# Four of the mixer's norms: squares added by block transposes on DVE and one 33-column matmul, 1 / rms on 32 partitions, spread by way of DRAM

## The chip, the cores and the metric

The kernel runs on one core of a Trainium2 chip. Its time is the device time of one execution in microseconds; the median of three runs was 1979.41 us. The engines are TensorE (PE; its weight loads are shown apart as PEld), VectorE (DVE), ScalarE (ACT), GpSimd (POOL) and SyncE (SP). In this kernel SP issues nearly all DMAs, from one queue in order.

## What is computed

One step of a decoder layer over 16 meta tokens, 1024 prompt tokens and 8 sample tokens, 1048 in all: a SwiGLU half step, a mixer of two head groups, an output projection, a second SwiGLU half step, a final norm. The change is in the mixer, in the norm of each HGRN2 head (four heads of 128 channels) and of each Mamba-2 group (two groups of 256 channels), cut from the reference:

```python
    o_hg = o_hg * lax.rsqrt(jnp.mean(o_hg * o_hg, axis=-1, keepdims=True) + EPS)
    o_hg = o_hg.reshape(bsz, seqlen, HG_WIDTH) * hg_norm.astype(f32) * jax.nn.silu(g.astype(f32))
    ...
    yz = (y.reshape(bsz, seqlen, SSM_WIDTH) * jax.nn.silu(z.astype(f32))).reshape(bsz, seqlen, SSM_GROUPS, -1)
    yz = yz * lax.rsqrt(jnp.mean(yz * yz, axis=-1, keepdims=True) + EPS)
    yz = yz.reshape(bsz, seqlen, SSM_WIDTH) * ssm_norm.astype(f32)
    ...
    mix = jnp.concatenate([o_hg, yz], axis=-1).astype(h.dtype) @ w_out
```

## The kernel before

**Layout.** Channels lie on the 128 partitions and tokens along the free dimension, so each norm is a sum over partitions, wanted on every partition for 1032 tokens (the meta tokens are dropped; `TO` = 1032).

**A norm.** `hgrn_out` (L1816) gets one head's output in three pieces of PSUM (496, 512 and 24 tokens). ACT squares each into `v`, DVE multiplies each by the weight `hg_norm` and the gate `g` (L1823), then TensorE multiplies a matrix of ones with the squares, in f32 (L1828): that adds over the partitions and puts the sum on all 128. ACT scales the sum and adds eps (L1829). `rstd_wide` (L190) follows: ACT loads the table with Ln and Exp (L194), takes Ln and Exp in two halves (L199, L201), DVE makes one Newton step of three passes over 128 x 1032 (L202, L203, L204), and the result `r` multiplies the gated output (L1831). `ssm_norm` (L1571) does the same for a group of two 128-channel tiles: squares (L1576, L1577), their sum (L1578), three matmuls with ones of 344 columns (L1583), `rstd_wide`, two products (L1587).

**What runs beside it.** In the mixer TensorE's order is written by hand; that of the other engines is not, and is made when the program is built. Between the steps of a scan `fill(n)` puts n steps of the input projections on TensorE: a step is one block k of 128 rows, three f32r matmuls of 344 to 350 columns (L163, L164, L165). The projections come as units in the order "q0 f0 v0 g0 q1 f1 v1 g1 z0 q2 f2 v2 g2 q3 f3 v3 z1 g3" of 24 steps each (48 for z0 and z1), 480 in all; `until(name)` runs steps until a unit is done, one step more than its last. When a unit begins, the weights of the one behind it are loaded by SP (L145, 256 KB each) and split by ACT and DVE.

**The order.** After the Mamba-2 scan, for each head hd: `fill.until("v{hd}")`, `fill(4)`, `hgrn_scan`, then for heads 0 to 2 `hgrn_out`. After head 0's come `until("z0")`, `fill(10)` and `ssm_norm` of group 0, then head 1's scan; so group 0's norm is followed by four steps of filler and a scan, and so is head 1's norm. After head 2's norm come the steps up to the end of v3 and four more. The norms of group 1 and of head 3 come at the end of the mixer. Normed outputs of heads 0 and 1 and of group 0 are written to DRAM (L2071) and read back late (L2075).

**The scan's beginning.** `hgrn_scan` transposes v on TensorE (L1650), ACT copies it (L1651), its last 8 tokens go to DRAM (`vd`, L1658) and come back spread over all partitions (L1670), for the samples' states (L1673, L1674). DVE makes q times f (L1686); TensorE makes the diagonal blocks (L1696), DVE copies them through a mask (L1700). Then come seven levels: small matmuls (L1725, from the sixth level up L1716), five filler steps, and DVE passes over q and k (L1747, L1748, L1750) on which the next level's matmuls wait. The transposes of k (L1768) follow.

Of the kernel before, what the change touches and what calls it, by code (L numbers as in the profile page):

```python
# [17 lines left out]
P = 128  # L18
D = 1024
KT = D // P  # L20
NM = 16
SEQ = 1024
TP = NM + SEQ
NS = 8
# [7 lines left out]
TO = T - NM  # L32
CHUNKS_O = [(NM, 344), (NM + 344, 344), (NM + 688, 344)]
CW = 350
SW = 1056
# [154 lines left out]
def rstd_wide(K, v, r, after):  # L190

    nc = K.nc
    with K.tc.issue_after(after.ins):
        ld = nc.scalar.preload_act_table_set("natural_log_exp_and_others")  # L194
    with K.tc.issue_after(ld.ins):
        n = v.shape[1] // 2
        parts = [(v[:, s : s + n], r[:, s : s + n]) for s in (0, n)]
        for vp, rp in parts:
            nc.scalar.activation(rp, vp, AF.Ln)  # L199
        for vp, rp in parts:  # L200
            nc.scalar.activation(rp, rp, AF.Exp, scale=-0.5, bias=K.lna)  # L201
        nc.vector.tensor_mul(v, v, r)  # L202
        nc.vector.scalar_tensor_tensor(v, v, -1.0, r, ALU.mult, ALU.mult)  # L203
        nc.vector.scalar_tensor_tensor(r, v, 3.0 * 2.0 ** (-2.0 / 3.0), r, ALU.add, ALU.mult)  # L204
# [325 lines left out]
class Inner:  # L530
# [10 lines left out]
    def next(self):  # L541
        return Inner(self.K, self.ops, self.op)
# [515 lines left out]
def constants_mix(K, a):  # L1058
    nc = K.nc
    cst = K.const  # L1060

    K.st, K.st0 = K.pack(), K.pack("u")

    K.tri = cst.tile([P, P], F32, name="tri")
    nc.gpsimd.affine_select(K.tri, K.ones[1], pattern=[[1, P]], compare_op=ALU.is_ge, fill=0.0, base=0, channel_multiplier=-1)

    K.mid = cst.tile([P, 32], U8, name="mid")
    for r in range(0, P, 32):
        nc.gpsimd.tensor_copy(K.mid[r : r + 32], K.ident[r : r + 32, r : r + 32])
    K.mask = {}  # L1070
    for m in LEVELS[:5]:
        nb = 64 // m
        f = K.sml.tile([P, 64], F32, tag="mf", name=K.uid("mf"))
        fv = f.rearrange("p (b i) -> p b i", i=m)
        on = K.ones[1][:, :64].rearrange("p (b i) -> p b i", i=m)

        nc.gpsimd.affine_select(fv, on, pattern=[[-2 * m, nb], [0, m]], compare_op=ALU.is_ge, fill=0.0, base=0, channel_multiplier=1)
        nc.gpsimd.affine_select(fv, fv, pattern=[[2 * m, nb], [0, m]], compare_op=ALU.is_ge, fill=0.0, base=m - 1, channel_multiplier=-1)
        u = cst.tile([P, 16], U8, name=f"mask{m}")
        for r in range(0, P, 32):  # L1080
            nc.gpsimd.tensor_copy(u[r : r + 32], f[r : r + 32, r // 2 : r // 2 + 16])
        K.mask[m] = u


    l0, l1 = K.pc["lb_logits"][:, 0:4], K.pc["lb_logits"][:, 4:8]
    e = K.st0.tile([P, 12])
    nc.vector.tensor_max(e[:, 8:12], l0, l1)
    nc.vector.tensor_sub(e[:, 0:4], l0, e[:, 8:12])
    nc.vector.tensor_sub(e[:, 4:8], l1, e[:, 8:12])
    nc.scalar.activation(e[:, 0:8], e[:, 0:8], AF.Exp)  # L1090
    nc.vector.tensor_add(e[:, 8:12], e[:, 0:4], e[:, 4:8])
    nc.vector.reciprocal(e[:, 8:12], e[:, 8:12])
    K.lb = cst.tile([P, 4], F32, name="lb")
    K.oml = cst.tile([P, 4], F32, name="oml")
    nc.vector.tensor_mul(K.lb, e[:, 0:4], e[:, 8:12])
    nc.vector.tensor_scalar(K.oml, K.lb, -1.0, 1.0, ALU.mult, ALU.add)

    K.dtb = K.st.tile([P, 8])
    nc.sync.dma_start(K.dtb, a["dt_bias"].to_broadcast([P, 8]))
    K.an = K.st.tile([P, 8])  # L1100
    nc.sync.dma_start(K.an, a["a_log"].to_broadcast([P, 8]))
    nc.scalar.activation(K.an, K.an, AF.Exp)
    nc.vector.tensor_scalar_mul(K.an, K.an, -1.0)
    K.dcol = K.st.tile([P, 4])
    for hf in range(2):
        nc.sync.dma_start(K.dcol[64 * hf : 64 * hf + 64, :], a["d_skip"].rearrange("l (j f) -> f l j", f=2)[hf].to_broadcast([64, 4]))

    K.sel16 = cst.tile([16, 8], F32, name="sel16")
    s2 = K.sml.tile([16, 8], F32, tag="s2", name="s2", bufs=1)
    nc.gpsimd.affine_select(K.sel16, K.ones[1][:16, :8], pattern=[[-1, 8]], compare_op=ALU.is_equal, fill=0.0, base=0, channel_multiplier=1)  # L1110
    nc.gpsimd.affine_select(s2, K.ones[1][:16, :8], pattern=[[-1, 8]], compare_op=ALU.is_equal, fill=0.0, base=-8, channel_multiplier=1)
    nc.gpsimd.tensor_add(K.sel16, K.sel16, s2)
# [455 lines left out]
    return f"z{g}", [wv[:, :, C_Z + i * P : C_Z + (i + 1) * P] for i in (2 * g, 2 * g + 1)], begin, [(i, c) for c in CHUNKS_O for i in range(2)]  # L1568


def ssm_norm(K, g, tag, fill):  # L1571

    nc = K.nc
    ya, yb = (K.y[2 * g + i][:, NM:] for i in range(2))
    v, r = K.slot(tag, w=TO), K.slot(tag, w=TO)
    nc.scalar.activation(v, ya, AF.Square)  # L1576
    nc.scalar.activation(r, yb, AF.Square)  # L1577
    nc.vector.tensor_add(v, v, r)  # L1578
    fill(10)
    for c0, w in CHUNKS_O:  # L1580
        cs = slice(c0 - NM, c0 - NM + w)
        ps = K.psm()[:, :w]
        nc.tensor.matmul(ps, K.ones[1], v[:, cs], start=True, stop=True)  # L1583
        an = nc.scalar.activation(v[:, cs], ps, AF.Identity, scale=1.0 / 256, bias=K.eps)
    rstd_wide(K, v, r, an)
    for i, y in enumerate((ya, yb)):
        nc.vector.scalar_tensor_tensor(y, y, K.pc["ssm_norm"][:, 2 * g + i : 2 * g + i + 1], r, ALU.mult, ALU.mult)  # L1587

# [227 lines left out]
def hgrn_out(K, hd, pieces, g, tag, fill):  # L1816

    nc = K.nc
    v, r = K.slot(tag, w=TO), K.slot(tag, w=TO)
    for ps, c0, w in pieces:  # L1820
        cs = slice(c0, c0 + w)
        nc.scalar.activation(v[:, cs], ps[:, :w], AF.Square)
        nc.vector.scalar_tensor_tensor(g[:, cs], ps[:, :w], K.pc["hg_norm"][:, hd : hd + 1], g[:, cs], ALU.mult, ALU.mult)  # L1823
    fill(5)
    for ps, c0, w in pieces:
        cs = slice(c0, c0 + w)
        pr = K.psm()
        nc.tensor.matmul(pr[:, :w], K.ones[1], v[:, cs], start=True, stop=True)  # L1828
        an = nc.scalar.activation(v[:, cs], pr[:, :w], AF.Identity, scale=1.0 / P, bias=K.eps)  # L1829
    rstd_wide(K, v, r, an)  # L1830
    nc.vector.tensor_mul(g, g, r)  # L1831


# [108 lines left out]
def body(ctx, tc, a, o):  # L1942
# [122 lines left out]
    ffn(K, a["w_ffn1_gate"][0], a["w_ffn1_up"][0], a["w_ffn1_down"][0], ops, spread, from1, first1, after1, 26)  # L2065

    constants_mix(K, a)
    md = K.dram.tile([D // 2, TO], F32, name="mspill")

# [18 lines left out]
    with K.tc.manual_schedule(engines={mybir.EngineType.PE}):  # L2088
# [178 lines left out]
```

## Time and profile before

| | |
|---|---|
| median of three runs | 1979.41 us (1973.97, 1979.57, 1979.41) |
| the profiled execution | 1973.32 us, its span 1971.5 us |
| granted TensorE clock, mean | 0.994 |
| busy in the span: PE, DVE, ACT, POOL | 98%, 78%, 44%, 4% |
| L1583, one matmul instruction of 344 columns | 0.45 us, 6 to a norm |
| L1828, of 496, 512 and 24 columns | 6 to a norm |
| DMA over the span | 258.45 MB, 131 GB/s |

A row of the profile gives the start in microseconds from the span's start, the duration, the engine, the line, the operation, what it writes and reads, and how many instructions the row holds; in brackets is the idle time of the engine before it and what ended that. A row of the chain gives start, length, engine, tile and line. An f32 matmul is run as two instructions. Matmuls overlap, so the distance from one start to the next tells more than a duration.

### The profile page before, as it was taken

To read this page: it belongs to the slowest core of one execution; us is meant where nothing else is said; L and a number is where in the kernel's file an instruction comes from. 1 tells how busy PE (TensorE), PEld (TensorE's weight loads), DVE (VectorE), ACT (ScalarE), POOL (GpSimd) and SP (SyncE) were. 2 spreads that over 40 slices of the span, in tenths; PEclk is the share of its full clock that TensorE was granted. 3 is DMA by queue.
4 is the path that set the end of the run, shared out by engine and by line. 5 is a ranking of instruction groups with operands and counts; after the bars stand their busy time and mean duration, and the time that the engine had idled before them with its cause. 6 is when DMAs were issued, how large, how long until landed. Compare 5 with 4: busy or idle time off the path is not lost.

```text
span 1971.5 us, 40943 instructions
## 1 busy us (share of the span) xinstructions
PE 1923.6 (98%) x16585; PEld 1885.4 (96%) x16585; DVE 1529.7 (78%) x2720; ACT 859.9 (44%) x1647; POOL 82.7 (4%) x135
## 2 busy tenths in 40 slices
PE   7999999999999999999999999999999999999997
PEld 6999999999999999998988989999999999999997
DVE  7788888888788776675755557888888888878973
ACT  7533232324534555465644535752332333354352
POOL 4000000000001310000000001200000000000000
PEclk9999999999999999999999999999999999999999
DMA  7233333335976632222522153224332333587851
GB/s 220 77 98 97 98 107 96 108 93 171 302 240 214 184 117 61 69 88 73 167 82 72 61 169 126 85 82 119 92 108 87 103 103 112 160 251 230 275 178 68
DMA packets 323877, 258.45 MB, mean 131 GB/s; under 512 B 17568, under 2 KB 299424, under 8 KB 323680
## 3 DMA queue, kind: packets, MB, share of 16 engines
q1 hardware_dynamic: 323448, 255.79, 42.1%
q8 instruction: 131, 2.15, 0.4%
q14 instruction: 58, 0.48, 0.1%
q0 software_dynamic: 224, 0.04, 0.0%
q10 hardware_dynamic: 16, 0.00, 0.0%
HBM read 190.79 MB, written 65.05 MB: 130 GB/s over the span
## 4 chain that ended last, share of the span: by engine, by line
PE 87%; DVE 7%; ACT 2%; DMA 2%; issue 1%; POOL 0%; SPq 0%; DVEq 0%; ACTq 0%; POOLq 0%
PE acc L163 26%; PE acc L165 26%; PE acc L164 26%; PE mis L163 1%; PE mis L165 1%; PE mis L164 1%; DVE u L352 1%; DMA s<-in_x_prompt_dram 1%; PE mis L1725 1%; PE mis L1449 0%; PE mis L1782 0%; DVE ws L466 0%; PE mis L1445 0%; DVE u L341 0%; DVE t L301 0%
## 5 line engine op out<-in xcount | busy, mean ns | idle before, releaser
L163 PE MATMUL acc<-u,ws 128*128 128x258 f32 (+3 forms) x4248 | 1242.9, 293 | 6.7 <-ACT t L674 1.7
L164 PE MATMUL acc<-u,ws 128*128 128x258 f32 (+3 forms) x4248 | 1232.1, 290 | 2.9 <-DVE u L352 2.7
L165 PE MATMUL acc<-u,ws 128*128 128x258 f32 (+3 forms) x4248 | 1231.1, 290 | 3.5 <-DVE ws L466 3.4
L163 PEld LDWEIGHTS acc<-u,ws 128*128 128x128 f32 x4248 | 803.9, 189 | 12.2 <-ACT t L674 2.1
L164 PEld LDWEIGHTS acc<-u,ws 128*128 128x128 f32 x4248 | 806.5, 190 | 5.8 <-DVE u L352 4.0
L165 PEld LDWEIGHTS acc<-u,ws 128*128 128x128 f32 x4248 | 803.6, 189 | 5.2 <-DVE ws L466 4.8
L466 DVE TENSOR_TENSOR ws<-r,ws 128x512 fp32r<-128x512 f32 x276 | 190.6, 691 | 75.0 <-ACT ws L462 74.9
L462 ACT CAST ws<-r 128x512 fp32r<-128x512 f32 x276 | 160.1, 614 | 13.3 <-ACT ws L462 7.8
L458 DVE TENSOR_TENSOR r<-r,r 128x512 f32<-128x512 f32 x176 | 121.5, 692 | 2.7 <-DMA r<-in_w_ffn_up_dram 1.2
L681 ACT ACTIVATE t<-t 128x516 f32<-128x516 f32 (+1 forms) x41 | 26.2, 639 | 212.9 <-DVE t L669 212.9
L712 ACT ACTIVATE t<-t 128x524 f32<-128x524 f32 (+1 forms) x47 | 29.9, 639 | 196.1 <-DVE t L669 196.1
L846 DVE TENSOR_TENSOR u<-u,u 128x1048 fp32r<-128x1048 f32 (+3 forms) x84 | 97.0, 1156 | 5.3 <-ACT u L842 4.5
L669 DVE TENSOR_TENSOR t<-t,u 128x524 f32<-128x524 f32 (+1 forms) x135 | 92.9, 697 | 2.8
L230 POOL TENSOR_TENSOR t<-t,t 128x262 f32<-128x262 f32 (+1 forms) x56 | 54.4, 981 | 823.6 <-ACT t L229 820.4
L158 DVE TENSOR_TENSOR ws<-r,ws 128x512 fp32r<-128x512 f32 x88 | 60.5, 698 | 36.0 <-ACT ws L157 35.6
L903 ACT CAST ws<-u 128x512 fp32r<-128x512 f32 (+1 forms) x72 | 42.2, 586 | 103.2 <-DVE u L898 100.2
L932 DVE SCALAR_TENSOR_TENSOR s<-acc,s 128x524 f32<-128x524 f32 (+3 forms) x88 | 54.6, 643 | 36.9 <-PE acc L165 36.5
L842 ACT CAST u<-u 128x1048 fp32r<-128x1048 f32 (+3 forms) x84 | 82.8, 988 | 0.0
L908 DVE TENSOR_TENSOR ws<-r,ws 128x512 fp32r<-128x512 f32 (+1 forms) x84 | 57.6, 693 | 22.3 <-ACT ws L903 22.2
L903 ACT CAST ws<-r 128x512 fp32r<-128x512 f32 (+1 forms) x84 | 47.9, 582 | 61.6 <-DVE r L898 37.0
L157 ACT CAST ws<-r 128x512 fp32r<-128x512 f32 x88 | 53.7, 618 | 35.6 <-PE acc L165 30.6
L908 DVE TENSOR_TENSOR ws<-u,ws 128x512 fp32r<-128x512 f32 (+1 forms) x72 | 47.4, 658 | 26.8 <-ACT ws L903 26.8
(417 smaller groups left out, 2297.9 us busy)
## 6 DMA issues: line engine op xcount, KB each, us to landing
r<-in_w_ffn_down_dram SPq DMA_DIRECT2D x128, 256.0 KB
hd<-s SPq DMA_DIRECT2D x93, 258.0 KB
r<-in_w_ffn_gate_dram SPq DMA_DIRECT2D x88, 256.0 KB
r<-in_w_ffn_up_dram SPq DMA_DIRECT2D x88, 256.0 KB
hd<-s SPq DMA_DIRECT2D x77, 262.0 KB
u<-hd SPq DMA_DIRECT2D x36, 516.0 KB
u<-hd SPq DMA_DIRECT2D x28, 524.0 KB
r<-in_w_in_dram SPq DMA_DIRECT2D x56, 256.0 KB
```

Source lines behind the costliest of these rows:

```text
L158: self.nc.vector.tensor_sub(lo, src, hi.bitcast(F32))
L163: mm(ps, whi, xhi, start=first, stop=False, skip_group_check=more)
L164: mm(ps, whi, xlo, start=False, stop=False, skip_group_check=more)
L165: mm(ps, wlo, xhi, start=False, stop=last, skip_group_check=more)
L458: self.K.nc.vector.tensor_tensor(self.raw[p], self.raw[x], self.raw[y], op)
L462: self.K.nc.scalar.copy(self.w[p][:, : self.n * P], self.raw[p])
L466: self.K.nc.vector.tensor_sub(t[:, 512 : 512 + w], self.raw[p], t[:, :w].bitcast(F32))
L669: nc.vector.tensor_mul(t, t if src is None else src, spread.lanes(i, cs))
L842: K.nc.scalar.copy(hi, lo.bitcast(F32))
L846: K.nc.vector.tensor_sub(lo, lo.bitcast(F32), hi.bitcast(F32))
L903: nc.scalar.copy(w[p, j, g][:, : n * P], src)
L908: nc.vector.tensor_sub(t[:, 512 : 512 + n * P], box[0], t[:, : n * P].bitcast(F32))
```

## The change

Head 0's, 1's and 2's norm and that of group 0 take another way, `norm_rows`; head 3's and group 1's stay. The squares lie in a tile of 128 x 1056, the last 24 columns set to zero. DVE transposes it in blocks of 32 x 32, so that within each group of 32 partitions a partition stands for a token of a block, and adds up the 32 entries of each block: 128 x 33 sums remain, each over 32 channels. One f32 matmul with `four` (four 32 x 32 unit matrices under each other) adds the four groups of partitions: 32 x 33, token i of block b at partition i, column b. The rest of the norm, ACT's scale, table load, Ln and Exp and DVE's Newton step, runs on that. DVE transposes the result back, two stores write it to DRAM as a row of 1032 numbers, and one load spreads the row to 128 partitions as `r`. The products with `r` are as before. The filler between squares and matmul goes from 10 steps to 16 in group 0 and from 5 to 14 in the three heads, and in `hgrn_out` the three products with `hg_norm` come after the transpose and the reduce.

```diff
+    K.four = cst.tile([P, 32], F32, name="four")
+    for r in range(0, P, 32):
+        nc.gpsimd.tensor_copy(K.four[r : r + 32], K.ident[r : r + 32, r : r + 32])
...
+def norm_rows(K, v, r, inv, fill):
+
+    nc = K.nc
+    a = K.t(192).rearrange("p (i b) -> p i b", i=3)
+    nc.gpsimd.memset(a[:32, 2], 0.0)
+    nc.gpsimd.memset(v[:, TO:], 0.0)
+    nc.vector.transpose(r, v)
+    nc.vector.tensor_reduce(a[:, 0, :33], r.rearrange("p (b j) -> p b j", j=32), mybir.AxisListType.X, ALU.add)
+    yield
+    ps = K.psm()
+    nc.tensor.matmul(ps[:32, :33], K.four, a[:, 0, :33], start=True, stop=True)
+    w, e = a[:32, 1, :33], a[:32, 2, :33]
+    an = nc.scalar.activation(w, ps[:32, :33], AF.Identity, scale=inv, bias=K.eps[:32])
+    with K.tc.issue_after(an.ins):
+        ld = nc.scalar.preload_act_table_set("natural_log_exp_and_others")
+    with K.tc.issue_after(ld.ins):
+        nc.scalar.activation(e, w, AF.Ln)
+        nc.scalar.activation(e, e, AF.Exp, scale=-0.5, bias=K.lna[:32])
+        nc.vector.tensor_mul(w, w, e)
+        nc.vector.scalar_tensor_tensor(w, w, -1.0, e, ALU.mult, ALU.mult)
+        nc.vector.scalar_tensor_tensor(e, w, 3.0 * 2.0 ** (-2.0 / 3.0), e, ALU.add, ALU.mult)
+    nc.vector.transpose(a[:32, 0], a[:32, 2])
+    d = K.dram.tile([1, SW], F32, name=K.uid("nr"))
+    nc.sync.dma_start(d[:, :1024].rearrange("o (b i) -> (o b) i", i=32), a[:32, 0, :32])
+    nc.sync.dma_start(d[:, 1024:TO], a[:1, 0, 32 : 32 + NS])
+    nc.sync.dma_start(r[:, :TO], d[:, :TO].to_broadcast([P, TO]))
...
 def ssm_norm(K, g, tag, fill):
...
+    if g == 0:
+        steps = norm_rows(K, vw, rw, 1.0 / 256, fill)
+        next(steps)
+        fill(16)
+        next(steps, None)
+    else:
+        fill(10)
...
 def hgrn_out(K, hd, pieces, g, tag, fill):
...
+    for ps, c0, w in pieces:
+        nc.scalar.activation(v[:, c0 : c0 + w], ps[:, :w], AF.Square)
+    if hd < 3:
+        steps = norm_rows(K, vw, rw, 1.0 / P, fill)
+        next(steps)
     for ps, c0, w in pieces:
         cs = slice(c0, c0 + w)
-        nc.scalar.activation(v[:, cs], ps[:, :w], AF.Square)
         nc.vector.scalar_tensor_tensor(g[:, cs], ps[:, :w], K.pc["hg_norm"][:, hd : hd + 1], g[:, cs], ALU.mult, ALU.mult)
-    fill(5)
...
+    if hd < 3:
+        fill(14)
+        next(steps, None)
+    else:
+        fill(5)
```

More of the change, by code (lines that the diff above doesn't have):

```diff
@@ L1574, in ssm_norm @@
     ya, yb = (K.y[2 * g + i][:, NM:] for i in range(2))
-    v, r = K.slot(tag, w=TO), K.slot(tag, w=TO)
+    vw, rw = K.slot(tag), K.slot(tag)
+    v, r = vw[:, :TO], rw[:, :TO]
     nc.scalar.activation(v, ya, AF.Square)
@@ L1578, in ssm_norm @@
     nc.vector.tensor_add(v, v, r)
[L1579 to L1585, printed above, removed]
+    if g == 0:
[5 more added lines that the diff above has]
+        fill(10)
+        for c0, w in CHUNKS_O:
+            cs = slice(c0 - NM, c0 - NM + w)
+            ps = K.psm()[:, :w]
+            nc.tensor.matmul(ps, K.ones[1], v[:, cs], start=True, stop=True)
+            an = nc.scalar.activation(v[:, cs], ps, AF.Identity, scale=1.0 / 256, bias=K.eps)
+        rstd_wide(K, v, r, an)
     for i, y in enumerate((ya, yb)):
@@ L1818, in hgrn_out @@
     nc = K.nc
-    v, r = K.slot(tag, w=TO), K.slot(tag, w=TO)
+    vw, rw = K.slot(tag), K.slot(tag)
+    v, r = vw[:, :TO], rw[:, :TO]
+    for ps, c0, w in pieces:
[3 more added lines that the diff above has]
+        next(steps)
     for ps, c0, w in pieces:
         cs = slice(c0, c0 + w)
-        nc.scalar.activation(v[:, cs], ps[:, :w], AF.Square)
         nc.vector.scalar_tensor_tensor(g[:, cs], ps[:, :w], K.pc["hg_norm"][:, hd : hd + 1], g[:, cs], ALU.mult, ALU.mult)
-    fill(5)
[L1825 to L1830, printed above, removed]
+    if hd < 3:
[3 more added lines that the diff above has]
+        fill(5)
+        for ps, c0, w in pieces:
+            cs = slice(c0, c0 + w)
+            pr = K.psm()
+            nc.tensor.matmul(pr[:, :w], K.ones[1], v[:, cs], start=True, stop=True)
+            an = nc.scalar.activation(v[:, cs], pr[:, :w], AF.Identity, scale=1.0 / P, bias=K.eps)
+        rstd_wide(K, v, r, an)
     nc.vector.tensor_mul(g, g, r)
```

## The prediction

> **What bounds the kernel now.** I read the page first: the engines' busy time, then the shares of the chain that ended last. TensorE is busy for 98% of the span and holds 87% of the chain.
>
> ```profile
> PE 1923.6 (98%) x16585; PEld 1885.4 (96%) x16585; DVE 1529.7 (78%) x2720; ACT 859.9 (44%) x1647; POOL 82.7 (4%) x135
> PE 87%; DVE 7%; ACT 2%; DMA 2%; issue 1%; POOL 0%; SPq 0%; DVEq 0%; ACTq 0%; POOLq 0%
> ```
>
> So a microsecond of TensorE work taken out of the mixer is a microsecond off the end, unless TensorE then waits. The second view is that chain in order of time, cut to the mixer (start, length, what). The squares are added by L1583 (`ssm_norm` of group 0) and L1828 (`hgrn_out` of heads 0, 1, 2). All four stand in it.
>
> ```profile
> 964.45 1.82 PE mis L1828 x6
> ...
> 1005.56 1.75 PE mis L1583 x6
> 1007.33 0.55 ACT s L1584
> 1007.90 1.28 ACT L194
> 1009.19 1.16 ACT s L199 x2
> 1010.35 1.24 ACT s L201 x2
> 1011.62 1.24 DVE s L202
> 1012.88 1.23 DVE s L203
> 1014.12 1.17 DVE s L1686
> 1015.42 1.13 PE mis L1725 x64
> ...
> 1059.06 2.06 PE mis L1828 x4
> ...
> 1110.86 1.82 PE mis L1828 x6
> ```
>
> After the second of them the chain leaves TensorE: eviction, table load, Ln, Exp, two Newton steps on DVE, and only then L1686, the product q·f on which the next head's first triangle matmuls (L1725) wait. After the third (1059.06) it is the same. The norm's own arithmetic holds up the scan behind it, through the queues of ACT and DVE. The third view is TensorE's timeline at the starts of the scans of heads 1 and 2, with the wait before each group in brackets.
>
> ```profile
> 1013.88 0.21 PE L1697 MATMUL mis<-u,u 128*16 128x16 f32 x2 [1.45 <-ACT s L1651]
> 1015.42 1.05 PE L1725 MATMUL mis<-s,u 128*32 128x16 f32 x64 [1.32 <-DVE s L1686]
> ...
> 1067.38 0.21 PE L1697 MATMUL mis<-u,u 128*16 128x16 f32 x2 [0.98 <-DVE t L1700]
> 1069.74 0.94 PE L1725 MATMUL mis<-s,u 128*32 128x16 f32 x61 [2.15 <-DVE s L1686]
> ```
>
> Those waits are 1.45 + 1.32 and 0.98 + 2.15. What they cost in all is seen by cutting the same piece out of each of the four scans, from its first transposes (L1650) to the transposes after its levels (L1768); the columns are the stretch, its length, busy time of PE, PEld, DVE, ACT, POOL, granted clock, DMA share and GB/s.
>
> ```profile
> 917.70:948.10 30.40, 27.99 (x569) 26.01 (x568) 20.62 (x60) 16.69 (x41) 0.00 (x0) 0.94 0.56 159
> 1009.00:1041.50 32.50, 28.66 (x570) 26.44 (x569) 25.88 (x56) 17.14 (x38) 0.00 (x0) 0.95 0.40 116
> 1063.00:1094.30 31.30, 28.18 (x570) 26.02 (x569) 23.21 (x50) 15.76 (x35) 0.00 (x0) 0.95 0.51 145
> 1130.80:1158.80 28.00, 26.63 (x569) 24.58 (x568) 19.83 (x49) 11.32 (x27) 0.00 (x0) 1.00 0.39 115
> ```
>
> The same 569 or so matmuls take 28.0 us for head 3, whose norm ahead is 20 us away, but 32.5 for head 1 and 31.3 for head 2, which have a norm four filler steps ahead. I take 4.5 + 3.3 = 7.8 us as what the two norms cost the scans behind them, idle time and lower clock together.
>
> **TensorE's part of the change.** Removed: 1.82 + 1.75 + 2.06 + 1.82 = 7.45 us. Added: four times one f32 matmul of 33 columns and 32 weight columns, two instructions. The nearest rows are these, and the row of the filler behind them.
>
> ```profile
> 959.81 0.40 PE L1808 MATMUL mis<-s,s 128*128 128x16 f32 x2
> 960.06 1.93 PE L1811 MATMUL mis<-qs,r 128*128 128x1 f32 x16
> 961.84 0.41 PE L163 MATMUL acc<-u,ws 128*128 128x344 f32 x1
> ...
> 964.28 1.99 PE L1828 MATMUL mis<-s,ones 128*128 128x496 f32 x6
> ```
>
> Two instructions of 16 columns hold TensorE for 960.06 - 959.81 = 0.25 us; sixteen of one column for 1.78, so 0.22 for two: the lower bound. The upper is a third of L1583, 0.58. I take 0.30, nearest the 16-column row: 1.2 us for four. Net -6.25 us. The filler total doesn't change: 480 steps, and "until v3" brings head 3's scan to step 413 either way. From 961.84 to 964.28 five steps take 2.44, so a step is 0.49 us.
>
> **Does the new matmul wait for its input?** In `hgrn_out` the last piece's matmuls end with L1811 (960.06 + 1.93 = 962.0) and its square, 0.19 long, runs at 962.02 (row further down), so the squares stand after 0.2 us; then come the block transpose and the reduce of 128x1056 on DVE. No row shows either. The nearest rows are DVE passes over 1032 columns:
>
> ```profile
> 1065.74 1.23 DVE L202 TENSOR_TENSOR s<-s,s 128x1032 f32<-128x1032 f32 x1 [9.87 <-ACT s L201]
> 962.24 0.24 DVE L1823 SCALAR_TENSOR_TENSOR u<-mis,col,u 128x24 f32<-128x24 f32 x1 [0.31 <-ACT s L1822]
> ```
>
> Each is bounded by 1.23 below and twice that above; I take 1.26. So the input stands after 0.2 + 2.5 = 2.7 us (5.1 at the upper bound), and fill(14) covers 14 x 0.49 = 6.9 us: free even at the upper bound. For group 0 fill(16) is 7.8 us against an add of 1.23 and the two passes. Without this cover it would be up to 6 us each. The three products with `hg_norm` now stand behind transpose and reduce on DVE, so three of four PSUM "mis" banks are held 2.5 us longer; the only taker before the next scan is the 33-column matmul, which uses the fourth. Nothing.
>
> **ACT, DVE, POOL.** Gone from ACT per norm are the wide eviction, Ln and Exp, and in their place stand three 33-column forms; the table load stays.
>
> ```profile
> 1062.02 1.28 ACT L194 ACT_TABLE_LOAD   x1
> 1063.31 1.16 ACT L199 ACTIVATE s<-s 128x516 f32<-128x516 f32 x2
> 1064.38 1.33 ACT L201 ACTIVATE s<-s,lna 128x516 f32<-128x516 f32 x2
> 962.02 0.19 ACT L1822 ACTIVATE s<-mis 128x24 f32<-128x24 f32 x1 [0.86 <-PE mis L1811]
> ```
>
> With 0.19 for a narrow form, ACT is held 0.19 + 1.28 + 0.38 = 1.85 us after the matmul instead of the 5.5 from 1007.33 on, so L1651 is no longer late. DVE loses 3 x 1.23 = 3.7 and gains 2.5 + 4 x 0.24 = 3.5: no less work, but 2.5 of it moves ahead of the matmul, under the filler, and L1686 has no wide Newton step before it. The four copies for `four` run on POOL, 4% busy, long before the mixer needs it; uncovered, under 1 us. The two memsets likewise, 0.1 each.
>
> **The moved steps.** 9, 6, 9 and 9 filler steps now run before the norm's matmul instead of behind it. Group 0's go from step 251 to 267 and cross 264, so unit f2 begins there and v2's two weight loads enter SP's queue ahead of the norm's three DMAs, not behind them; head 2's scan now ends at step 385 instead of 370, so v3 begins and z1's four loads go out ahead of its norm. Heads 0 and 1 (173 to 187, 319 to 333) cross no unit. All are earlier than before, so no weight is late by it.
>
> **The new wait: r comes by DRAM.** After the narrow ACT steps come three narrow DVE steps and a transpose, about 0.96 us, so 2.8 us after the matmul the two stores can be issued. SP then waits for them and issues the broadcast load of 128 x 4128 bytes. The kernel already does this in small: `vd` is stored and read back to all partitions, in 256 KB loads.
>
> ```profile
> 1132.83 0.29 SPq L1658 DMA_DIRECT2D vd<-vs  x1
> 1134.09 0.33 SPq L1670 DMA_DIRECT2D r<-vd  x1
> ...
> 1138.16 1.28 ACT L1673 ACTIVATE r<-r,qs 128x128 f32<-128x128 f32 x4 [3.59 <-DMA r<-vd]
> ...
> 1170.47 6.97 DMA u<-mspill
> ACT r L1673 <- DMA r<-vd: 14.6, 5, 4.1
> ```
>
> Store to load is 1.26 us (1134.09 - 1132.83), with 0.33 for the second store; a 256 KB broadcast lands 4.07 us after its issue (1138.16 - 1134.09), and a 516 KB load in a busy stretch 6.97. r's load lies between; I take 5.0. So r stands 2.8 + 1.6 + 5.0 = 9.4 us after the matmul. Before, behind L203 at 1012.88 came L1686 and the last Newton step, so r stood at 1012.88 + 1.23 + 1.17 + 1.23 = 1016.5, 9.2 us after the matmuls' end at 1007.31: r is no earlier. But until then DVE is free for the scan, if the multiply that needs r isn't queued ahead of the scan's steps. The order on DVE, ACT and SP isn't written by hand here. Behind a blocked multiply stand the scan's L1747 and L1748, on which the next L1725 waits. The last row is how the like load is met today: ACT waits for it five times, 14.6 us in all, 4.1 at most; eight were issued. I call B the time for which DVE stands blocked on r.
>
> The Trainium skill, "DMA: Bandwidth & Descriptors", section "Anatomy of one DMA", puts a fixed cost of about 2 us on every transfer, most of it the receipt from the written memory, which speaks against two trips in a row. By its fit an estimate is 2.0 for the store and 2.0 + 528384 B / 436 GB/s = 3.2 for the load, 5.2 against my 6.6, so r at 8.0 and B shorter by 1.4. The rows show a cheaper store and a dearer load, and the sum goes by the rows.
>
> One level has 5 filler steps, 2.4 us, against 1.2 of DVE work that it must wait for, so 1.2 us of a block is hidden. Head 1's scan gets group 0's two products (2 x 1.23) and loses 1.3 + B; head 2's gets one and loses B; head 3's scan starts 14 steps (6.9 us) after the matmul and loses B - 1.5. Head 0's norm is followed by over 50 steps of filler and loses nothing. B's bounds are 0 and about 7; five waits of mean 2.9 among eight loads give 1.8, and I take 2. Then 3.3 + 2 + 0.5 = 5.8 us are lost where 7.8 were.
>
> **Sum.** -6.25 - 7.8 + 5.8 = -8.2 us. The profiled execution took 1973.3 (span 1971.5 and 1.8 around it), so 1965.1 by its measure; it lies at the low end of the runs (1973.97 to 1979.57), and against their median, 1979.4, it is 1971.2.
>
> **The rivals.** (a) B is 0, as the multiply falls behind r's landing in DVE's order: 1.3 lost, -6.25 - 6.5 = -12.7, 1966.7. For it: r comes at the time it came before, so an order like the old one has no block. Against it: the waits of ACT on r<-vd.
> (b) B is 4.1, the longest of those waits: 5.4 + 4.1 + 2.6 = 12.1 lost against 7.8, so -6.25 + 4.3 = -1.9, 1977.5: the stall moves from arithmetic to DMA and eats most of the gain.
> (c) Slower: the broadcast gets the busy stretch's 6.97 us, since the 516 KB sit in one queue with w_in, state and r<-vd loads, and the multiply stands early in DVE's order, B = 7: 8.3 + 7 + 5.5 = 20.8, +13.0 - 6.25 = +6.8, 1986.2. It decides from the point where the three losses pass 7.8 + 6.25 = 14.05, that is B = 4.75; past B = 6.7 it is measurable. For it: SP is in order, and the load waits there for both stores. Against it: DMA share is 0.40 to 0.51 in these two scans.
> (d) The change doesn't do what it says, the 33-column matmul waiting beyond its filler: covered above; it is inside (b).
>
> The lower clock is inside the 7.8. Where waits remain it may remain:
>
> ```profile
> 1012.00:1016.00 4.00, 1.23 (x96) 1.05 (x86) 3.96 (x4) 3.88 (x7) 0.00 (x0) 0.91 0.00 1
> 1016.00:1020.00 4.00, 4.00 (x52) 3.79 (x44) 3.84 (x5) 0.34 (x1) 0.00 (x0) 0.67 0.59 170
> ```
>
> 0.09 x 4 + 0.33 x 4 = 1.7 us of clock were lost behind a stretch in which TensorE worked 1.23 of 4 us. The Trainium skill, "TensorE: Matmul & The Clock Gate", section "Part 1: The HAM clock gate", halves the clock after an idle window of some 3.4 us; by that rule a single 2 us wait would cost no clock, while the trace has it lost behind two waits of 1.45 and 1.32.
>
> **Chances.** The forecast 0.50, its own range 1966 to 1976; (a) 0.14; (b) with (d) 0.21; (c) 0.15. What a measurement of this kernel can tell from no change is about 0.3%, 5.9 us. Of the forecast 0.42 lies beyond that; with (a) faster is 0.56. Same is 0.08 + 0.21 = 0.29, slower 0.15. The range goes down to (a) less the runs' own spread of 5, 1962, and up past (b) to 1981; it leaves out (c) alone.
>
> **What would show it.** Right: two-instruction norm matmuls of 33 columns at 0.25 to 0.4 us with no wait; L1651's copy and L1686's product without a wait of TensorE behind them; the stretches of heads 1 and 2 at 29 to 31 us. Wrong: a wait of DVE on the broadcast above 4 us with L1725 idle behind it, head 3's stretch well above 28, weight casts waiting for w_in loads behind the norm's stores on SP, or the new matmul idle behind the transposes.

## The result, and the profile after

| | median us | lowest to highest | runs | ratio to before, 95% |
|---|---|---|---|---|
| before | 1978.43 | 1973.78 to 1985.46 | 12 | |
| after | 1968.08 | 1962.65 to 1973.70 | 12 | 0.9945 [0.9934, 0.9957] |

The changed kernel is faster by 10.9 us (0.0055 x 1978.4), between 8.5 and 13.1 by the interval. The forecast was -8.2 and 1971.2 us; rival (a), in which DVE never stands blocked on r, was -12.7 and 1966.7. The time lies between the two, nearer to (a).

The profiled execution of after took 1968.44 us (span 1966.7), that of before 1973.32. The pair shows only 4.9 us, because before's lies below all of its 12 runs and because after's mean granted clock was 0.991 against 0.994. So the pair is read in the piece of the mixer that holds all four norms, from the first transposes of head 0's scan to those behind the levels of head 3's. The columns are the stretch, its length, busy time of PE, PEld, DVE, ACT and POOL with counts, granted clock, DMA share and GB/s; first before, then after.

```profile
917.70:1158.80 241.10, 230.37 (x3044) 217.07 (x3043) 143.72 (x371) 119.93 (x260) 3.94 (x11) 0.97 0.36 105
```

```profile
920.50:1152.30 231.80, 223.53 (x3026) 213.12 (x3025) 142.71 (x383) 109.37 (x245) 4.72 (x17) 0.97 0.41 119
```

Here 9.3 us are gone: 6.8 of TensorE's busy time (230.37 - 223.53) and 2.5 of its idle time (10.73 - 8.27). ACT lost 10.6 us of work, DVE 1.0. The rest of the page stays as it was: TensorE 98% busy and most of the chain.

```profile
PE 1923.2 (98%) x16569; PEld 1888.5 (96%) x16569; DVE 1529.4 (78%) x2732; ACT 850.4 (43%) x1632; POOL 85.2 (4%) x147
PE 88%; DVE 7%; ACT 2%; DMA 2%; issue 1%; POOL 0%; SPq 0%; DVEq 0%; ACTq 0%; POOLq 0%
```

The four scans of after, cut as in the prediction (same columns; in order heads 0 to 3):

```profile
920.50:952.20 31.70, 29.20 (x568) 27.06 (x567) 20.47 (x60) 16.71 (x41) 0.00 (x0) 0.89 0.56 148
1014.80:1045.80 31.00, 28.20 (x569) 26.22 (x568) 23.37 (x57) 14.29 (x34) 0.00 (x0) 0.94 0.52 155
1068.60:1097.70 29.10, 26.78 (x568) 24.66 (x566) 19.72 (x51) 17.23 (x34) 0.00 (x0) 1.00 0.56 165
1125.50:1152.30 26.80, 26.14 (x568) 24.27 (x566) 20.55 (x50) 11.36 (x27) 0.00 (x0) 1.00 0.45 139
```

Against before, heads 1, 2 and 3 went from 32.5, 31.3 and 28.0 to 31.0, 29.1 and 26.8, 4.9 us less. Head 0's scan, which has no changed norm ahead, went up by 1.3 at a lower clock (0.89 for 0.94). A second profiled execution of the same kernel (the run `e10_after_again` below) has these for heads 1 to 3, 6.6 us less than before:

```profile
1010.00:1040.30 30.30, 28.25 (x567) 26.23 (x566) 23.32 (x57) 14.13 (x34) 0.00 (x0) 0.94 0.53 159
1064.70:1092.70 28.00, 26.63 (x568) 24.57 (x567) 19.56 (x51) 16.87 (x34) 0.00 (x0) 1.00 0.59 172
1120.50:1147.40 26.90, 26.18 (x569) 24.29 (x567) 20.59 (x50) 11.31 (x27) 0.00 (x0) 1.00 0.44 138
```

Measured as the prediction did, against 28.0 for each, 2.9 and 1.2 us are lost in these three scans where it forecast 5.8.

Where head 1's scan still loses is seen in the new norm ahead of it. The timeline of after, TensorE, ACT, DVE and SP put one behind the other (start, duration, engine, line, operation, shapes; in brackets the wait before):

```profile
1012.62 0.25 PE L1585 MATMUL mis<-t,four 128*32 128x33 f32 x2
...
1012.96 0.28 ACT L1587 ACTIVATE t<-mis,eps 32x33 f32<-32x33 f32 x1 [1.23 <-PE mis L1585]
1013.26 1.28 ACT L1589 ACT_TABLE_LOAD   x1
1014.56 0.23 ACT L1591 ACTIVATE t<-t 32x33 f32<-32x33 f32 x1
1014.82 0.33 ACT L1592 ACTIVATE t<-t,lna 32x33 f32<-32x33 f32 x1
...
1015.58 1.22 DVE L1725 TENSOR_TENSOR s<-u,u 128x1040 f32<-128x1040 f32 x1
1016.83 0.68 DVE L1789 TENSOR_TENSOR s<-u 128x520 f32<-128x520 f32 x1
1017.44 0.23 DVE L1596 STREAM_TRANSPOSE t<-t 32x64 f32<-32x64 f32 x1
...
1017.69 0.32 SPq L1598 DMA_DIRECT2D nr<-t  x1
1018.06 0.28 SPq L1599 DMA_DIRECT2D nr<-t  x1
1019.36 1.10 SPq L1600 DMA_DIRECT2D s<-nr  x1
...
1025.28 2.50 DVE L1626 SCALAR_TENSOR_TENSOR u<-u,col,s 128x1032 f32<-128x1032 f32 x2 [0.64 <-DMA s<-nr]
...
1028.21 0.21 PE L1776 MATMUL mis<-s,u 128*16 128x8 f32 x2 [2.70 <-DVE p L1779]
```

The matmul ends at 1012.87, the stores go out at 1017.69, the load at 1019.36, and r stands at 1025.28: 12.4 us, not 9.4. Yet DVE waited for it only 0.64, since the two products with r (L1626) came late in its order, behind the work of the scan's first levels. Then they ran for 2.50 us, a mask copy of the level (L1779) came behind them, and TensorE stood 2.70, nearly all of its idle time in this scan (31.00 - 28.20 = 2.80). The waits of 1.45 and 1.32 at this scan's beginning are gone. At the beginning of head 2's, where 0.98 and 2.15 stood, after has these on TensorE (1.5 us more of its idle time there have no cause in the profile):

```profile
1072.48 0.21 PE L1736 MATMUL mis<-u,u 128*16 128x16 f32 x2 [0.51 <-ACT s L1690]
1072.96 0.70 PE L1764 MATMUL mis<-s,u 128*32 128x16 f32 x62 [0.26 <-ACT s L1690]
```

In the second execution, `e10_after_again`, r had landed before DVE came to the two products in head 1's scan, so DVE was not blocked at all. TensorE still stood 1.97 us behind them:

```profile
1019.82 2.49 DVE L1626 SCALAR_TENSOR_TENSOR u<-u,col,s 128x1032 f32<-128x1032 f32 x2
...
1022.74 0.21 PE L1776 MATMUL mis<-s,u 128*16 128x8 f32 x2 [1.97 <-DVE p L1779]
```

So most of TensorE's wait of 2.70 in after is the run time of the products ahead of the mask copy, and the rest is the block of 0.64.

### The profile page after: what moved, and what is told of

It is laid out like the page before. It is cut to its first block, busy times and chain, and to the rows that moved or that the text cites. A ratio compares the mean times of both kernels' runs of the same rounds, so it can differ in the third digit from the quotient of the medians.

```text
span 1966.7 us, 40940 instructions
## 1 busy us (share of the span) xinstructions
PE 1923.2 (98%) x16569; PEld 1888.5 (96%) x16569; DVE 1529.4 (78%) x2732; ACT 850.4 (43%) x1632; POOL 85.2 (4%) x147
## 3 DMA queue, kind: packets, MB, share of 16 engines
q8 instruction: 131, 2.15, 0.5%
## 4 chain that ended last, share of the span: by engine, by line
PE 88%; DVE 7%; ACT 2%; DMA 2%; issue 1%; POOL 0%; SPq 0%; DVEq 0%; ACTq 0%; POOLq 0%
PE acc L163 26%; PE acc L165 26%; PE acc L164 26%; PE mis L163 1%; PE mis L165 1%; PE mis L164 1%; DVE u L352 1%; DVE ws L466 1%; DMA r<-vd 1%; DVE u L341 1%; PE mis L1453 0%; PE mis L1764 0%; PE mis L1821 0%; PE mis L1449 0%; DVE u L846 0%
```

## The experiments

Each kernel was timed in five rounds against the kernel before. "After" in an edit means that the changed kernel was edited, "before" that the old one was.

| label | median us | ratio, 95% | us against before |
|---|---|---|---|
| e1_fill_only | 1981.23 | 1.0018 [1.0008, 1.0029] | +3.6 |
| e2_no_trip | 1960.39 | 0.9918 [0.9904, 0.9931] | -16.2 |
| e3_heads_0_2 | 1972.27 | 0.9972 [0.9961, 0.9984] | -5.5 |
| e4_group0_head1 | 1971.29 | 0.9971 [0.9962, 0.9980] | -5.7 |
| e5_narrow_matmul | 1971.65 | 0.9963 [0.9949, 0.9976] | -7.3 |
| e6_old_fill | 1965.10 | 0.9937 [0.9918, 0.9956] | -12.5 |
| e7_late_product | 1965.18 | 0.9930 [0.9909, 0.9950] | -13.8 |
| e8_late_product_7 | 1964.65 | 0.9928 [0.9912, 0.9943] | -14.2 |
| e9_two_trips | 1969.07 | 0.9965 [0.9951, 0.9978] | -6.9 |
| e10_after_again | 1967.73 | 0.9956 [0.9943, 0.9969] | -8.7 |
| e11_late_product_7_again | 1963.95 | 0.9931 [0.9919, 0.9943] | -13.6 |

The last column is (ratio - 1) times the before of the same comparison (1977.4 to 1977.7). e5 to e8 ran on another chip than e1 to e4 and e9 to e11, so kernels of the two groups are compared by their ratios. The two readings of the unedited kernel, -10.9 and -8.7, show how far one such number can be trusted.

To see more than a median gives, I cut each profiled execution as the pair above and split the stretch: idle is its length less PE busy, lost clock is each window of 2 us times (1 - granted clock), summed, and the rest is TensorE's work at full clock.

| kernel | stretch | lost clock | idle | rest |
|---|---|---|---|---|
| before | 241.1 | 6.8 | 10.7 | 223.5 |
| after | 231.8 | 6.8 | 8.3 | 216.7 |
| e10 (after again) | 229.1 | 5.1 | 6.7 | 217.3 |
| e1 | 244.1 | 8.6 | 12.8 | 222.8 |
| e2 | 225.3 | 3.4 | 4.3 | 217.6 |
| e3 | 242.3 | 8.5 | 13.4 | 220.4 |
| e4 | 238.9 | 10.2 | 8.7 | 220.0 |
| e5 | 235.7 | 6.8 | 11.4 | 217.5 |
| e6 | 231.2 | 6.9 | 6.8 | 217.5 |
| e7 | 231.2 | 6.8 | 7.2 | 217.2 |
| e8 | 227.7 | 3.4 | 6.7 | 217.6 |
| e9 | 233.0 | 6.8 | 9.6 | 216.6 |
| e11 | 228.2 | 3.4 | 7.1 | 217.7 |

The rest is steady: 223 with four wide norms (before, e1), 220 with two (e3, e4), 217 with none; among the nine rows with none it lies between 216.6 and 217.7, so one cell is good to about 1 us. Lost clock comes in steps of 1.7 us whose number differs between executions of one kernel (after and e10). Idle time was expected to repeat within 0.5 us in e10, and did not: 8.3 and 6.7 for the same kernel. So a difference of 2 us between two cells of the idle column shows little by itself.

### TensorE's part alone: e5_narrow_matmul

On the kernel before, for the four norms; nearly all of the sums over partitions are left out:

```diff
-        pr = K.psm()
-        nc.tensor.matmul(pr[:, :w], K.ones[1], v[:, cs], start=True, stop=True)
-        an = nc.scalar.activation(v[:, cs], pr[:, :w], AF.Identity, scale=1.0 / P, bias=K.eps)
+        if hd == 3 or w == 24:
+            pr = K.psm()
+            nc.tensor.matmul(pr[:, :w], K.ones[1], v[:, cs], start=True, stop=True)
+            an = nc.scalar.activation(v[:, cs], pr[:, :w], AF.Identity, scale=1.0 / P, bias=K.eps)
+        else:
+            an = nc.scalar.activation(v[:, cs], v[:, cs], AF.Identity, scale=1.0 / P, bias=K.eps)
```

Group 0 likewise, with 33 columns of its last piece.

> The kernel before, with the matmuls with ones of the four norms cut to one of 33 columns (group 0) or to the 24-column piece (heads 0 to 2); ACT's scaling reads the squares themselves elsewhere, so the sums are left out and the normed outputs are wrong, but ACT's and DVE's wide steps, the filler counts and their order stay. It measures TensorE's part by itself: my sum has 6.2 us for it, so 5 to 8 us faster than before (0.25 to 0.4%). A rival in which TensorE's work was hidden behind the waits of the next scan gives under 3 us. The other rival, that the moved or shrunk work on ACT and DVE is worth nothing, gives here all of the change's 10.9 us.

Measured: -7.3 us, between -4.7 and -10.1 by the interval, and the rest falls from 223.5 to 217.5. The scans behind the norms keep their losses (heads 1 and 2; before had 32.5 and 31.3):

```profile
1004.90:1039.00 34.10, 29.99 (x568) 27.71 (x567) 25.91 (x56) 17.44 (x36) 0.00 (x0) 0.90 0.35 110
1057.50:1088.60 31.10, 26.90 (x568) 24.68 (x567) 23.41 (x50) 15.24 (x34) 0.00 (x0) 1.00 0.53 146
```

So TensorE's term is shown by itself, 6.0 to 6.8 us by the rest (223.5 less 217.5 or 216.7). What the change gains beyond it is not shown by the times, since -7.3 and the unedited kernel's -10.9 and -8.7 have overlapping intervals. By the traces it is idle time, 11.4 us in e5 against 8.3 and 6.7, and all idle time of before and of after lies inside the four scans.

### The filler alone: e1_fill_only

```diff
-    fill(10)
+    fill(16 if g == 0 else 10)
-    fill(5)
+    fill(14 if hd < 3 else 5)
```

> The kernel before with the new filler counts alone (16 and 14 steps ahead of the norms' matmuls, which stay wide with ones). My theory, that the gain is TensorE work taken out (6.4 us) plus less of the norm's arithmetic in the queues ahead of the scans of heads 1 and 2, gives no gain here: between 0.3% slower and 0.3% faster, and from the first transposes of head 0's scan to the last of head 3's (241 us before, 232 after the change) between 239 and 243 us. The rival that the longer cover makes the gain gives a time within 3 us of the changed kernel and a stretch of 232 to 235 us.

Measured: +3.6 us, within the expected 0.3%, but the interval excludes no change, and the stretch of 244.1 us lies just outside the expected 239 to 243. The rival, that the longer cover makes the gain, is out. Of the 3 us by which the stretch is longer than before's, 2.1 are idle time and 1.7 one more step of lost clock, while the rest is 0.7 less. The number of steps varies between executions of one kernel as well (after and e10). The prediction called these moved steps free, since no weight is late by them. Head 1's scan in e1 takes 34.0 us for 32.5 before:

```profile
1012.80:1046.80 34.00, 29.09 (x568) 26.93 (x567) 24.99 (x55) 16.30 (x38) 0.00 (x0) 0.90 0.43 126
```

Its timeline, DVE first and then the TensorE row on which it ends:

```profile
1020.61 2.49 DVE L1587 SCALAR_TENSOR_TENSOR u<-u,col,s 128x1032 f32<-128x1032 f32 x2
1023.02 0.69 DVE L1747 TENSOR_TENSOR s<-s,u 128x520 f32<-128x520 f32 x1
1023.63 0.69 DVE L1748 TENSOR_TENSOR u<-u,u 128x520 f32<-128x520 f32 x1
...
1024.47 1.06 PE L1725 MATMUL mis<-s,u 128*32 128x16 f32 x64 [4.77 <-ACT r L1673]
```

In before the products stood between the two, and TensorE's wait behind L1748 was 0.32:

```profile
1016.57 0.70 DVE L1747 TENSOR_TENSOR s<-s,u 128x520 f32<-128x520 f32 x1 [0.16 <-PE mis L1725]
1017.19 2.49 DVE L1587 SCALAR_TENSOR_TENSOR u<-u,col,s 128x1032 f32<-128x1032 f32 x2
1019.60 0.69 DVE L1748 TENSOR_TENSOR u<-u,u 128x520 f32<-128x520 f32 x1
```

So DVE's order was made anew, and it now puts the norm's two products (L1587) ahead of both L1747 and L1748; TensorE stands 4.77 us. The profile names ACT's L1673 as what ended the wait, which had itself waited for the load of `vd`. But the matmuls read what L1747 and L1748 write, and they start 0.15 us after L1748 ends, as they do in before (1019.60 + 0.69 = 1020.29, start at 1020.44). That speaks for DVE; no run separates the two. What is shown is that moving filler changed another engine's order, and that the kernel took longer although no wait of TensorE for a weight stands in this stretch.

### Less filler in the new norm: e6_old_fill

```diff
-        fill(16)
+        fill(10)
-        fill(14)
+        fill(5)
```

> The changed kernel with the filler counts of before (10 and 5 steps between squares and matmul). Since the new counts alone cost the old kernel 3.6 us, one theory gives 2 to 4 us faster than the changed kernel. The other: the sums stand 2.9 us after the last piece's matmuls (head 1: L1850 ends at 1059.8, the reduce at 1062.7) and five steps cover 2.4, so TensorE waits 0.5 to 1 us in each of three heads, and the time is the changed kernel's or up to 3 us more.

Measured: -12.5 us, not to be told from after, so the time decides between neither theory. With 5 steps the new matmul waited in one norm of four:

```profile
1105.52 0.25 PE L1585 MATMUL mis<-t,four 128*32 128x33 f32 x2 [0.42 <-DVE t L1582]
```

So the longer cover buys at most 0.42 us here, and what e1 lost by it is not seen in the changed kernel.

### Two norms of the four: e3_heads_0_2 and e4_group0_head1

```diff
-    if g == 0:
+    if g < 0:
-    if hd < 3:
+    if hd in (0, 2):
```

is e3; e4 keeps group 0 and has `if hd in (1,):`.

> The new norm in heads 0 and 2 alone; group 0 and head 1 as before. These two have 10 steps of filler or more behind them, so my theory leaves only TensorE's part: 2 x (1.82 - 0.25) = 3.1 us, 0.16%, and a stretch of about 238 us. The rival that all four gain alike gives half of the whole, 5 us and a stretch of 236.5 us.

> The new norm in group 0 and head 1 alone; heads 0 and 2 as before. TensorE's part is 1.75 + 2.06 - 0.5 = 3.3 us; to it come the waits at the starts of the scans of heads 1 and 2, of which my theory has 2 to 5 us come back: 5 to 8 us in all and a stretch of 233 to 236 us. The rival that all four gain alike gives 5 us and 236.5 us; the rival that the trip by DRAM eats the waits' gain gives 3.3 us or less and 238 us.

Measured: -5.5 and -5.7, together about what the whole change gives. By the medians the gain is spread evenly, as the rival has it; e3's interval reaches from -3.2 to -7.7 and so just holds the 3.1 of the theory. e3's stretch of 242.3 fits neither (238 and 236.5), and e4's 238.9 lies above the 233 to 236 expected. The traces say more: e3 has only TensorE's term (rest 220.4), and its idle time is no less than before's (13.4), with 33.90 - 27.25 = 6.65 of it in head 1's scan:

```profile
1010.40:1044.30 33.90, 27.25 (x567) 24.96 (x566) 25.80 (x56) 17.29 (x38) 0.00 (x0) 1.00 0.39 111
```

e4, which has the new norms ahead of heads 1 and 2, has 8.7 idle. Its profiled execution lost three steps of clock more than e10's, which hides that in one time.

### The trip by DRAM: e2_no_trip and e9_two_trips

e2 leaves out the two stores and the load, and so the numbers that the products need: r keeps the transposed squares.

```diff
-    d = K.dram.tile([1, SW], F32, name=K.uid("nr"))
-    nc.sync.dma_start(d[:, :1024].rearrange("o (b i) -> (o b) i", i=32), a[:32, 0, :32])
-    nc.sync.dma_start(d[:, 1024:TO], a[:1, 0, 32 : 32 + NS])
-    nc.sync.dma_start(r[:, :TO], d[:, :TO].to_broadcast([P, TO]))
```

> The changed kernel without the two stores and the broadcast load: r keeps the block-transposed squares, so the four normed outputs are multiplied by wrong numbers, and no multiply waits for DRAM. My theory puts what DVE's wait for r costs at 2 to 5 us (a wait of 0.6 us and two products on the path in head 1's scan, then half the clock for a window), so 2 to 5 us faster than the changed kernel and a stretch of 227 to 230 us. The rival that the trip is hidden anyway gives the changed kernel's time within 1 us and 231 to 232 us.

Measured: -16.2, and head 1's scan has no idle time at all:

```profile
1012.30:1038.70 26.40, 26.40 (x567) 24.53 (x566) 20.77 (x55) 13.98 (x34) 0.00 (x0) 1.00 0.45 122
```

That is 5.3 to 7.5 us better than after, more than the 2 to 5 expected (0.9918 against 0.9945 and 0.9956, times 1978), although in after the scans' DVE waited for the trip only 0.64. But e2 takes out more than the trip. Its products wait for nothing behind the transpose, and DVE runs them right behind the reduce, 7 us ahead of the norm's matmul (1010.08) and 9 us ahead of the scan:

```profile
1003.43 2.49 DVE L1622 SCALAR_TENSOR_TENSOR u<-u,col,s 128x1032 f32<-128x1032 f32 x2
```

So the 5.3 to 7.5 us are what the trip and the products' place in the scan cost together; e2 can't give the trip's price alone. e9 puts a second trip, DRAM to DRAM, ahead of the load:

```diff
-    nc.sync.dma_start(r[:, :TO], d[:, :TO].to_broadcast([P, TO]))
+    d2 = K.dram.tile([1, SW], F32, name=K.uid("nq"))
+    nc.sync.dma_start(d2[:, :1024].rearrange("o (b i) -> (o b) i", i=64), d[:, :1024].rearrange("o (b i) -> (o b) i", i=64))
+    nc.sync.dma_start(d2[:, 1024:TO], d[:, 1024:TO])
+    nc.sync.dma_start(r[:, :TO], d2[:, :TO].to_broadcast([P, TO]))
```

> The changed kernel with a second trip: the row of 1 / rms is copied once more within DRAM (two stores of 4 KB and 32 bytes) before the broadcast load, so r lands later by about one store, 1.3 us or more. My theory: DVE stands blocked on r that much longer in head 1's scan, and in head 2's and 3's where it was just covered, 2 to 6 us slower than the changed kernel. If the wait for the trip is hidden and only the DVE passes of the products cost, the same within 1.5 us.

Measured: 1969.07, 1.3 over the unedited kernel's 1967.73 beside it; the intervals overlap. The 2 to 6 us of the theory were not seen, and the other expectation, the same within 1.5 us, holds. DVE was blocked 0.34 in head 2's scan and not at all in head 3's. In head 1's scan of e9, DVE and then TensorE:

```profile
1026.99 2.50 DVE L1629 SCALAR_TENSOR_TENSOR u<-u,col,s 128x1032 f32<-128x1032 f32 x2 [1.86 <-DMA s<-nq]
...
1029.81 0.22 PE L1779 MATMUL mis<-s,u 128*16 128x8 f32 x2 [3.65 <-DVE p L1782]
```

With e10 and after that makes three traces of one place: a block of 0, 0.64 and 1.86 us, and a wait of TensorE of 1.97, 2.70 and 3.65. So a longer block reaches TensorE nearly whole, and about 2 us of the wait are there without any block.

### The products behind the levels: e7, e8 and e11

If what e2 gained lies in where the products with r stand, moving them behind the scan's seven levels should give it back with the trip kept.

```diff
-    for i, y in enumerate((ya, yb)):
-        nc.vector.scalar_tensor_tensor(y, y, K.pc["ssm_norm"][:, 2 * g + i : 2 * g + i + 1], r, ALU.mult, ALU.mult)
+    def products():
+        for i, y in enumerate((ya, yb)):
+            nc.vector.scalar_tensor_tensor(y, y, K.pc["ssm_norm"][:, 2 * g + i : 2 * g + i + 1], r, ALU.mult, ALU.mult)
+    return products
...
+    for fn in K.late:
+        fn()
+    K.late = []
...
-    nc.vector.tensor_mul(g, g, r)
+    return lambda: nc.vector.tensor_mul(g, g, r)
```

The caller appends what is returned, and the writes to DRAM behind it, to `K.late`; `hgrn_scan` runs the list behind its levels. Head 0's product runs at once. e8 has 10 and 7 steps of filler as well, and e11 is e8 again, beside the unedited kernel.

> The changed kernel with the products with r (and the stores of the normed outputs) of group 0, head 1 and head 2 put behind the seven levels of the next head's scan in the program, so that no multiply that waits for DRAM stands among the levels' steps on DVE. If the rest of the loss is that multiply (0.6 us of wait, 2.5 of products, then half the clock in head 1's scan, 2.3 us idle in head 2's), it comes to the time without the trip: 3 to 5 us faster than the changed kernel, 0.992 to 0.993 of before. If what the kernel without the trip gained was the load on the DMA queue (w_in, state and vd loads behind 528 KB), nothing is gained, 0.994 to 0.995.

> The late products, with 10 filler steps in group 0 and 7 in the heads between squares and matmul: 7 steps cover 3.4 us where 2.9 are needed. If the longer cover of the change costs 3.6 us for the units that it moves into other scans, this is 2 to 4 us faster than the late products alone; if those 3.6 us were a matter of the old norm, it is the same within 2 us.

> The changed kernel itself, on the chip and against the runs of the next one: 0.9945 of before as first measured, between 0.993 and 0.996. Its profile is a second execution of the same order: between the first transposes of head 0's scan and the last of head 3's the work and the idle time should repeat within 0.5 us, and the time lost to a lower clock may differ by whole steps of 1.7 us.

> The late products with 10 and 7 filler steps again, beside the changed kernel on one chip: if it beats both kernels, 2 to 5 us under the changed kernel, 0.992 to 0.9935 of before, with no wait of TensorE behind a product with r in the scans of heads 1 to 3.

Measured: -13.8, -14.2 and -13.6. On the same chip and in the same comparison e11 is 3.8 us under the unedited kernel (1963.95 for 1967.73); their intervals touch at 0.9943. All three are faster than the kernel before, and their medians lie under all those of the changed kernel, though e8's and e11's intervals overlap with its first one, and e7's with both.

How much of this the moved products give is open. e8 and e11 change the filler as well, and e6, which changes the filler alone, has a ratio of 0.9937 beside e7's 0.9930 and e8's 0.9928 in the same comparison: the three are not told apart. e7's interval, 0.9909 to 0.9950, holds both of its expectations. By the traces idle time is 7.2, 6.7 and 7.1 us, no less than e10's 6.7. That e8 is within 2 us of e7 is what was expected if the cost of the longer cover belonged to the old norm.

Heads 1, 2 and 3 in e11:

```profile
1010.60:1040.60 30.00, 27.07 (x569) 24.86 (x568) 22.26 (x56) 16.54 (x36) 0.00 (x0) 1.00 0.44 143
1060.10:1088.20 28.10, 26.37 (x568) 24.40 (x567) 19.53 (x50) 13.65 (x33) 0.00 (x0) 1.00 0.65 190
1122.30:1148.50 26.20, 26.18 (x569) 24.32 (x568) 19.70 (x49) 11.32 (x27) 0.00 (x0) 1.00 0.43 123
```

The group's products (L1627) ran from 1033.28 and 1035.77 on, near the end of the scan, and head 1's scan lost no clock (1.00 for after's 0.94). It still has 2.9 us idle where e2 has none. The profile puts 0.8 of them to ACT's copy of v (L1693), 0.5 to DVE's L1790, and names no cause for 1.7. By the ratios 2.0 to 2.6 us of e2's gain are not given back (-16.2 less -14.2 and -13.6).

## Why the prediction came out right, and where its sizes were off

The forecast was -8.2 and the two readings of the kernel are -10.9 and -8.7, so by the times alone the forecast and rival (a), -12.7, are not told apart: the first interval, 8.5 to 13.1, just leaves out the forecast, and the second, 6.1 to 11.3, leaves out (a). The terms are told apart by the traces.

**TensorE's part (-6.25).** Right: 6.0 to 6.8 by the rest, -7.3 by e5. A pair of 33-column matmuls took 0.25 us (forecast 0.30).

**The cover of transpose and reduce.** Right, and longer than needed. The DVE rows of group 0's norm in after:

```profile
1003.49 1.28 DVE L1581 STREAM_TRANSPOSE s<-s 128x1056 f32<-128x1056 f32 x1
1004.80 1.25 DVE L1582 TENSOR_REDUCE t<-s 128x33 f32<-128x1056 f32 x1
```

Both cost what a plain pass costs (1.26 each was taken). The matmul had no wait with 14 and 16 steps and 0.42 once with 5.

**ACT's narrow forms (0.19 each, ACT held 1.85).** The order of the size was right: 0.28, 0.23 and 0.33 us, 2.2 us from 1012.96 to 1015.15 instead of 5.5. Not foreseen was head 1's norm, where ACT's order put filler work with another table between Ln and Exp, two table loads that the prediction has not. ACT in after:

```profile
1068.32 0.23 ACT L1591 ACTIVATE t<-t 32x33 f32<-32x33 f32 x1
1068.57 1.28 ACT L1642 ACT_TABLE_LOAD   x1
1069.87 0.46 ACT L1642 ACTIVATE u<-acc 128x344 f32<-128x344 f32 x1
1070.35 1.28 ACT L1592 ACT_TABLE_LOAD   x1
1071.64 0.32 ACT L1592 ACTIVATE t<-t,lna 32x33 f32<-32x33 f32 x1
```

That made L1690's copy, queued behind, late by the 0.51 + 0.26 shown above, against the forecast that it would not be.

**When r stands (9.4 us behind the matmul).** Too early by 3: 12.4. Narrow steps 4.8 (forecast 2.8, because DVE's order puts the scan's L1725 and L1789, 1.22 + 0.68, among them), store to load 1.67 (1.6), load 5.9 (5.0). The Trainium skill, "DMA: Bandwidth & Descriptors", section "Anatomy of one DMA", which the prediction used beside its rows, fits its 2 us on DMAs that GpSimd issues, and these go by SP: 5.2 us for store and load by that fit, 6.6 by the sum, 7.6 measured (1.67 + 5.9).

**The block B (2 us) and the stalls' gain (2.0).** This is the term that was mis-sized. B was 0.64 in head 1's scan and nothing in those of heads 2 and 3; in e10 it was nothing, 1.16 and nothing; the row of the product of head 1's output, in the scan of head 2 there:

```profile
1079.50 1.23 DVE L1879 TENSOR_TENSOR u<-u,s 128x1032 f32<-128x1032 f32 x1 [1.16 <-DMA s<-nr]
```

r came later than forecast and DVE was blocked less, because the multiply stood later in its order than the prediction put it: the condition of rival (a). So the stalls gave 4.9 and 6.6 us in the two executions, in the prediction's own measure, and with TensorE's term that is -11.2 and -12.9. The whole stretch, head 0's scan included, went down by 9.3 and 12.0 (241.1 to 231.8 and 229.1). That the total of -8.2 is so near the measured -8.7 and -10.9 is therefore in part luck: by the traces the scans gave 2.9 and 4.6 us more than forecast, and the medians show less of that.

Not all of it is B. In after 0.3 of the 2.9 lie in head 1's scan, 0.9 in head 2's and 1.7 in head 3's, which was to lose 0.5 and gained 1.2. The base was too high: head 3's 28.0 us held 1.37 of idle time (28.00 - 26.63), so it was no scan without stalls; head 1's takes 26.4 in e2, and head 3's 26.2 in e11. Why head 3's scan got shorter was not tested.

What remained in head 1's scan is the run time of the products: 1.3 + 0.64 = 1.9 by the forecast's formula, which took 1.2 of them as hidden, 2.70 as TensorE waited (1.97 with no block, by e10, where the formula has 1.3), and a step of clock of 1.7 behind it.

The forecast's reason for choosing 2, ACT's five waits for the load of `vd`, was taken from another engine in another place of its queue; it says what such a load takes, not where the instruction that needs it will stand. Rivals (b) and (c) needed a B of 4.1 and 7. e9's trace shows their mechanism (1.86 of block, 3.65 of wait), but its time is not told apart from the unedited kernel's, and at the length of the single trip the block was 1.16 us at most in these three scans.

**The moved steps (nothing).** Wrong for the old kernel, +3.6 by e1, and most likely by a way that the prediction didn't look at: the order of the other engines. In the changed kernel no such cost was seen (e6).

## What to carry to other kernels

Where the orders of other engines are made when the program is built, the price of a late operand is set by where its consumer stands in that order: forecast the position first, then the latency. An edit that only moves filler can cost time (+3.6 us in e1). The consumer's own run time counts as well as its block: 1.97 us of TensorE's wait were left in e10 with no block at all. Moving such a consumer behind the loop is worth a try; here its gain was not separated from that of the filler. A wide sum over partitions by ones on a bound TensorE is well replaced by block transposes, a reduce and one narrow matmul, when a few filler steps cover the passes.

## What was not expected of the hardware

The clock is lost in whole steps, and not only behind idle time. The first two windows are after's, in head 1's scan. Then come before's, ahead of head 1's norm matmul, first TensorE's row and then the windows (columns as above):

```profile
1024.00:1028.00 4.00, 1.41 (x69) 1.05 (x67) 3.36 (x7) 1.17 (x3) 0.00 (x0) 1.00 0.97 300
1028.00:1032.00 4.00, 3.79 (x15) 3.77 (x16) 3.08 (x10) 1.80 (x5) 0.00 (x0) 0.57 0.98 326
```

```profile
1053.44 1.93 PE L1811 MATMUL mis<-qs,r 128*128 128x1 f32 x16
```

```profile
1052.00:1056.00 4.00, 4.00 (x34) 3.85 (x33) 1.54 (x3) 1.17 (x5) 1.03 (x3) 1.00 0.00 0
1056.00:1060.00 4.00, 4.00 (x14) 3.39 (x13) 0.00 (x0) 0.02 (x1) 0.00 (x0) 0.57 0.00 0
```

Each is a loss of 0.43 x 4 = 1.7 us. The first lies behind 4 us in which TensorE worked 1.41; in the second TensorE is busy for all of the 4 us and of the 4 before, and sixteen one-column matmuls had ended 0.6 us ahead of it (1053.44 + 1.93 = 1055.37). The Trainium skill, "TensorE: Matmul & The Clock Gate", section "Part 1: The HAM clock gate", has the clock halved for windows of about 3.4 us; half of that is 1.7, and the traces agree: each step is 1.7 us, and a 2 us window inside one has a clock of 0.50 (after, 1028.50 to 1030.50). It has that happen behind an idle window, and ahead of the second no idle time is shown. In the stretch of 225 to 244 us the kernels lost two to six such steps, and the same kernel three and four in two executions; a different number of steps is enough to account for part of the spread of 11 us among runs of one kernel. The recorded mean clocks fit that: of after's 12 runs the four with a clock of 0.993 or more took 1962.65 to 1964.53 us, the four with 0.990 or less 1968.90 to 1973.70. What decides their number was not found.
